# Start addresses of the tiles that TensorE reads, on multiples of 256 bytes, in a hybrid encoder block

## The chip, the core and the metric

The kernel runs on one core of one Trainium2 chip. The metric is the device time of one execution in microseconds, from runs of the whole kernel. The core has TensorE (PE, matmuls), VectorE (DVE), ScalarE (ACT), GpSimd (POOL) and SyncE (SP, which issues transfers). SBUF is the working memory: 128 partitions, each a run of bytes; a tile takes the same bytes in every partition. Matmuls write to PSUM. A matmul has a *stationary* operand, which a weight load (PEld in the profile) puts into the array, and a *moving* operand, which streams through it.

## The reference, cut to what matters

One layer on a sequence of 512 tokens with 1024 features, all in float32:

```
h      = rms_norm(x, g)
proj   = h @ w_in             # 1024 -> mLSTM q,k,v,o,gates | NA q,k,v | memory q | merge gates
y_ml   = mlstm_branch(...)                  # 4 heads of 128, two directions
y_na   = neighbourhood_attention(...)       # 8 heads of 64, an 8 x 64 grid
y_xa   = memory_cross_attention(...)        # 4 heads of 128, 256 memory tokens
merged = g_ml*(y_ml@w_br_ml) + g_na*(y_na@w_br_na) + g_xa*(y_xa@w_br_xa)
x      = x + merged @ w_out
x      = x + conv_glu_ffn(rms_norm(x), w_up, w_conv, b_conv, w_down)   # 1024 -> 2 x 2816 -> 1024
return rms_norm(x, final_norm_g)
```

Nearly all of the arithmetic is in the products with weights: `w_in`, the branch outputs, `w_out`, `w_up` and `w_down`.

## The kernel before

Activations are kept transposed: a tile holds 128 features by 512 tokens. For precision each float32 operand of a large product is split into a high part (`float32r`) and a low part, what is left; a product is then three matmuls, written by one helper, `mm3` (lines 207 to 209): high weights x high features, high weights x low features, low weights x high features. Each of the three loads its stationary operand anew.

Weights come in blocks of up to 1024 columns by a transfer into a `raw` tile (`wr`, three buffers), are split by ACT (line 189, high part) and DVE (line 190, low part) into tiles `wh` and `wl` (four buffers each, `HWD` = 544 floats a partition, that is 2176 bytes), one block ahead of TensorE. `proj` runs over the eight 128-feature slices of a contraction and calls `mm3` for each; the weights are stationary (128 x 128) and the features move (128 x 512). In the projection to mLSTM v and neighbourhood v (the blocks `tm`) and in the memory's v (`memv`) it is the other way: features or memory are stationary and weights move.

Features live in a ring of 15 `unit` buffers (`u`, `UNIT` = 2064 floats = 8256 bytes a partition), each with room for four tiles of 512. The input features, the merged features and those of the feed-forward stage take four units each. In all three, the first two units hold the high parts (eight tiles) and the last two the low parts, by lines such as

```
XH = [hx[k // 4][:, (k % 4) * S:(k % 4 + 1) * S] for k in range(KT)]
XL = [hx[2 + k // 4][:, (k % 4) * S:(k % 4 + 1) * S] for k in range(KT)]
```

Scratch tiles (`s`, seven buffers) are 516 floats. Constants (`ident` for transposes, `ones`, `onesr`) are single tiles in the pool `cp`. The row of norms, 512 reciprocal norms spread over all partitions (`rb_x` for the input, `rb_2` for the feed-forward stage, written at line 312), has two buffers. `rb_x` is read last in the gates of the third branch (line 1027).

The pools are laid out one behind the other in SBUF, in the order in which tiles are first made, on multiples of 32 bytes. So the sizes above decide at which byte each tile starts. The Tile framework orders each engine's work as the program is written.

Of the kernel before, what the change touches and what calls it, by code (L numbers as in the profile page):

```python
# [11 lines left out]
F32 = mybir.dt.float32  # L12
F32R = mybir.dt.float32r
# [4 lines left out]
P = 128  # L18
S = 512
D = 1024  # L20
KT = D // P
# [10 lines left out]
EPS = 1e-6  # L32
NEG = -1e30
BW = 1088
HWD = 544
UNIT = 2064
ROWS, GW = 8, 64
CW = (0, 8, 24, 32)
C_ML = (128.0 ** -0.5) / 4.0
# [67 lines left out]
def hybrid_block(ctx, tc, xg, xT, memT, wflat, vecs, gbias, nabias, outa, outb):  # L107
# [3 lines left out]
    cp = ctx.enter_context(tc.tile_pool(name="cp", bufs=1))  # L111
    wp = ctx.enter_context(tc.tile_pool(name="wp", bufs=3))
    up = ctx.enter_context(tc.tile_pool(name="up", bufs=NU))
    sp = ctx.enter_context(tc.tile_pool(name="sp", bufs=7))
# [7 lines left out]
    def nm(s):  # L122
        uid[0] += 1
        return f"{s}_{uid[0]}"

    def unit(dt=F32):
        return up.tile([P, UNIT], dt, tag="unit", name=nm("u"))

    def scr(n=512):
        return sp.tile([P, 516], F32, tag="scr", name=nm("s"))[:, :n]  # L130

    def tiny(n):
        return tp.tile([P, 32], F32, tag="tiny", name=nm("y"), bufs=12)[:, :n]
# [23 lines left out]
    def halves(i):  # L157
        n, c = BLOCKS[i][1], BCOLS[BLOCKS[i][0][0]](BLOCKS[i][0])
        k = n // c
        k0 = k if n <= HWD else (k + 1) // 2  # L160
        return c, [(0, k0)] + ([(k0, k)] if k0 < k else [])
# [10 lines left out]
    def emit_split(i):  # L172
        key, n = BLOCKS[i]
        r = raws.pop(i)
        c, hs = halves(i)
        split[i] = []
        for a, b in hs:
            m = (b - a) * c
            if key[0] == "dnl":
                h, l = lastw(4 * key[1] + a, m)  # L180
            else:
                h = wp.tile([P, HWD], F32R, tag="hi", name=nm("wh"), bufs=4)
                l = wp.tile([P, HWD], F32R, tag="lo", name=nm("wl"), bufs=4)
            for u, v in ((0, P), (P, 2 * P), (2 * P, m)) if i == 0 and a == 0 else ((0, m),):
                src = r[:, a * c + u:a * c + v]
                if i == 0 and a == u == 0:
                    V.tensor_copy(h[:, u:v], src)
                else:
                    A.activation(h[:, u:v], src, AF.Copy)  # L189
                V.tensor_tensor(l[:, u:v], src, h[:, u:v].bitcast(F32), op=ALU.subtract)  # L190
            for k in range(a, b):
                q = slice((k - a) * c, (k - a + 1) * c)
                split[i].append((h[:, q], l[:, q]))
# [62 lines left out]
    A.activation(cp.tile([P, 2], F32, name="first"), nc.const_aps.tensor(1.0, [P, 2], F32), AF.Tanh)  # L256
    SY.dma_start(vec, vecs)

    ident = cp.tile([P, P], F32, name="ident")
    make_identity(nc, ident)  # L260
    ones = cp.tile([P, P], F32, name="ones")
# [37 lines left out]
    def rstd_row(col, ntok, tag):  # L299

        nt = ntok // P
        ch, cl = tp.tile([P, 32], F32R, tag="tiny", name=nm("y"), bufs=12)[:, :nt], tiny(nt)
        A.activation(ch, col, AF.Copy)
        V.tensor_tensor(cl, col, ch.bitcast(F32), op=ALU.subtract)
        pb = atps()
        for n, c in enumerate((ch.bitcast(F32), cl)):
            dg = sp.tile([P, 516], F32R, tag="scr", name=nm("s"))[:, :ntok]
            for t in range(nt):
                V.tensor_scalar(dg[:, t * P:(t + 1) * P], ident, c[:, t:t + 1], None, op0=ALU.mult)
            PE.matmul(pb[:, :ntok], onesr, dg, start=n == 0, stop=n == 1)  # L310
        rb = cp.tile([P, ntok], F32, name=f"rb_{tag}", tag=f"rb{ntok}", bufs=2 if ntok == S else 1)
        A.activation(rb, pb[:, :ntok], AF.Copy)
        return rb


    hx = [unit(F32R) for _ in range(4)]
    XH = [hx[k // 4][:, (k % 4) * S:(k % 4 + 1) * S] for k in range(KT)]
    XL = [hx[2 + k // 4][:, (k % 4) * S:(k % 4 + 1) * S] for k in range(KT)]
    acc = cp.tile([P, S], F32, name="acc_x", tag="acc", bufs=1)

    ps_q = [mmps() for _ in range(4)]
# [1 line left out]
    def x_part(k):  # L323
        g = xgt[:, k:k + 1]
        if k > 0:
            split_act(XH[k], XL[k], xk[k], g)
        if k == 0:
            ha, hb = slice(0, S // 2), slice(S // 2, S)
            A.activation(XH[0][:, ha], xk[0][:, ha], AF.Copy, scale=g)
            A.activation(XH[0][:, hb], xk[0][:, hb], AF.Copy, scale=g)  # L330
        else:
# [37 lines left out]
    for k in range(KT):  # L369
# [75 lines left out]
    for c in range(3):  # L445
        n, nk = TMC[c], TMK[c]
        pss = [(mmps if c % 2 else atps)() for _ in range(NT)]
        for h in range(KT // nk):
            ws = weights(("tm", c, h))
            for t in range(NT):  # L450
                tsl = slice(t * P, (t + 1) * P)
                for k in range(nk):
                    kk = nk * h + k
                    ps = pss[t][:, :n]
                    mm3(ps, XH[kk][:, tsl], XL[kk][:, tsl], ws[k][0], ws[k][1], kk == 0, kk == KT - 1)
        for t in range(NT):
            ps = pss[t]
            if c == 0:
                V.scalar_tensor_tensor(Gt[:, t, :], ps[:, :16], rc[:, t:t + 1], gb, op0=ALU.mult, op1=ALU.add)
            if c < 2:  # L460
                o = 16 if c == 0 else 0
                A.activation(va[:, t, 2 * c:2 * c + 2, 0:128],
                             ps[:, o:o + 256].rearrange("p (h c) -> p h c", h=2), AF.Copy, scale=rcc[:, t:t + 1])
            if c > 0:

                nv = sp.tile([P, 516], F32R, tag="scr", name=nm("nv"))[:, :512]
                nvv = nv.rearrange("p (q y d) -> p q y d", q=2, y=4)
                pv = ps[:, n - 256:n].rearrange("p (q e d) -> p q e d", q=2, e=2)
                A.activation(nvv[:, :, 0:4:3, :], pv, AF.Copy, scale=rc[:, t:t + 1])
                for q in range(2):  # L470
                    V.scalar_tensor_tensor(nvv[:, q, 1:3, :], pv[:, q], rc[:, t:t + 1], nvv[:, q, 0:4:3, :].bitcast(F32),
                                           op0=ALU.mult, op1=ALU.subtract)
                G.dma_start(nav_d[t * P:(t + 1) * P, (c - 1) * 512:c * 512], nv)
# [389 lines left out]
    def xa_all(xq, mk, mv, yh, yl):  # L863
# [54 lines left out]
        q, k = prep(0)  # L918
        yield
        prev = None  # L920
        for h in range(4):
            sm = [scores(tq, q, k) for tq in range(2)]
            if prev:
                values(h - 1, *prev)
            yield
            v = prep_v(h)
            pT = [[sp.tile([P, 516], F32R, tag="scr", name=nm("s"))[:, :S] for _ in range(2)] for _ in range(2)]
            for tq in range(2):
                transposes(tq, sm[tq], pT)
            prev = (v, pT)  # L930
            if h < 3:
                q, k = prep(h + 1)
            yield
# [82 lines left out]
    for br in range(3):  # L1016
# [18 lines left out]
        for fp in range(4):  # L1035
# [6 lines left out]
            for i in range(2):  # L1042
                f = 2 * fp + i
# [8 lines left out]
                    V.tensor_tensor(mgv(f), mgv(f), tg[i], op=ALU.add)  # L1052
            step(RATE[br])
    mhu = [unit(F32R) for _ in range(4)]
    GH = [mhu[k // 4][:, (k % 4) * S:(k % 4 + 1) * S] for k in range(KT)]
    GL = [mhu[2 + k // 4][:, (k % 4) * S:(k % 4 + 1) * S] for k in range(KT)]
    for k in range(KT):
        split_act(GH[k], GL[k], mgv(k), 0.5)

# [1 line left out]
    x2u = [unit(), unit()]  # L1061
    x2 = [x2u[f // 4][:, (f % 4) * S:(f % 4 + 1) * S] for f in range(KT)]
    h2 = [unit(F32R) for _ in range(4)]
    HH = [h2[k // 4][:, (k % 4) * S:(k % 4 + 1) * S] for k in range(KT)]
    HL = [h2[2 + k // 4][:, (k % 4) * S:(k % 4 + 1) * S] for k in range(KT)]
    acc2 = cp.tile([P, S], F32, name="acc_2", tag="acc", bufs=1)
    for f in range(KT):
        xr = scr()
        SY.dma_start(xr, xT[f])
        ps = proj(("out", f), GH, GL)  # L1070
        V.tensor_tensor(x2[f], ps, xr, op=ALU.add)
        split_act(HH[f], HL[f], x2[f], vcol("ffn_g", f))
        if f == 0:
# [128 lines left out]
    for hh in range(2):  # L1202
# [159 lines left out]
```

## Time and profile before

| | |
|---|---|
| median of 3 runs | 896.2 us (895.94 to 896.33) |
| the profiled execution's own time | 895.66 us |
| its span, first to last instruction | 893.9 us |
| matmul instructions | 4350 |
| bytes moved by transfers | 99.68 MB |
| granted TensorE clock | 1.00 |

How to read it: busy time on TensorE is modelled, since matmuls are pipelined; two of them overlap in the profile, so that the mean of one is longer than the distance from one start to the next. `PEld` is the weight load, which runs beside the matmul before it. In the groups, a name such as `mm<-u,wh` says that a PSUM tile is written from a feature unit and a high weight tile; `x1022` is the count, then the busy time in us and the mean of one in ns.

### The profile page before, as it was taken

The page shows a single profiled execution, that of the slowest core. Times are in us where ns is not written, and L with a number is a line of the kernel's source. Part 1 is how long each engine was busy: PE and PEld are TensorE (multiplying, and loading weights), DVE is VectorE, ACT ScalarE, POOL GpSimd, SP SyncE. Part 2 cuts the span into 40 slices and gives each one's busy share as a digit, 9 for nine tenths or more (in the row PEclk, how much of TensorE's full clock was granted, in tenths as well). Part 3 has the DMA queues.
Part 4 walks back from the last instruction along what each step waited for, and adds up shares of the span by engine and source line. Part 5 has one row for each costly group of instructions (what it writes and reads, how often), then busy time and mean ns, then how long its engine had stood idle before and what let it go on. Part 6 is the DMA issues. An engine that isn't in the chain of part 4 may idle for free.

```text
span 893.9 us, 12254 instructions
## 1 busy us (share of the span) xinstructions
PE 887.6 (99%) x4350; PEld 741.5 (83%) x4350; DVE 578.1 (65%) x1181; ACT 451.7 (51%) x951; POOL 135.3 (15%) x209
## 2 busy tenths in 40 slices
PE   9999999999999999999999999999999999999997
PEld 7898889888888888888888888888888888888887
DVE  6794686766567657998676548766633566667433
ACT  7353556644556548888644435444422344444442
POOL 0101100000070660510000211111100011111010
PEclk9999999999999999999999999999999999999999
DMA  7224643422242443533223322222223222222412
GB/s 269 97 84 126 203 131 118 166 103 87 71 124 91 117 119 118 150 122 119 105 95 107 142 106 94 95 95 95 73 98 105 102 95 96 98 96 82 138 34 95
DMA packets 39293, 99.68 MB, mean 112 GB/s; under 512 B 5688, under 2 KB 14008, under 8 KB 39232
## 3 DMA queue, kind: packets, MB, share of 16 engines
q1 hardware_dynamic: 31440, 92.32, 30.0%
q0 software_dynamic: 7360, 6.32, 3.2%
q8 instruction: 34, 0.56, 0.3%
q10 hardware_dynamic: 432, 0.26, 0.1%
q14 instruction: 27, 0.22, 0.1%
HBM read 94.67 MB, written 4.21 MB: 111 GB/s over the span
## 4 chain that ended last, share of the span: by engine, by line
PE 98%; ACT 1%; issue 0%; DVE 0%; POOLq 0%; POOL 0%; DVEq 0%
PE mm L208 29%; PE mm L207 29%; PE mm L209 29%; PE at L207 2%; PE at L208 2%; PE at L209 2%; PE at L816 1%; PE at L670 1%; PE at L797 1%; PE at L635 1%; PE at L672 1%; PE at L651 0%; PE at L904 0%; PE at L779 0%; PE at L778 0%
## 5 line engine op out<-in xcount | busy, mean ns | idle before, releaser
L207 PE MATMUL mm<-u,wh 128*128 128x512 f32 (+1 forms) x1076 | 420.0, 390 | 0.0
L208 PE MATMUL mm<-u,wh 128*128 128x512 f32 (+1 forms) x1076 | 418.0, 388 | 0.0
L209 PE MATMUL mm<-u,wl 128*128 128x512 f32 (+1 forms) x1076 | 416.6, 387 | 0.0
L189 ACT ACTIVATE wh<-wr 128x512 fp32r<-128x512 f32 (+3 forms) x299 | 185.5, 622 | 266.8 <-PE mm L208 218.5
L190 DVE TENSOR_TENSOR wl<-wr,wh 128x512 fp32r<-128x512 f32 (+3 forms) x300 | 206.7, 690 | 110.7 <-ACT wh L189 106.0
L209 PEld LDWEIGHTS mm<-u,wl 128*128 128x128 f32 x1076 | 202.2, 188 | 43.5
L207 PEld LDWEIGHTS mm<-u,wh 128*128 128x128 f32 x1076 | 202.3, 188 | 42.7
L208 PEld LDWEIGHTS mm<-u,wh 128*128 128x128 f32 x1076 | 202.4, 188 | 42.0 <-DVE u L214 0.3
L1231 POOL TENSOR_TENSOR s<-s,rb 128x512 f32<-128x512 f32 x22 | 37.4, 1699 | 257.7 <-DVE s L1230 249.6
L483 POOL DMA_DIRECT2D u<-nav_d x128 | 62.5, 556 | 74.8 <-PE at L816 34.7
L213 ACT ACTIVATE u<-s 128x512 fp32r<-128x512 f32 x26 | 16.4, 631 | 53.8 <-DVE s L1234 53.6
L1234 DVE TENSOR_TENSOR s<-mm,s 128x512 f32<-128x512 f32 x22 | 15.2, 690 | 22.5 <-POOL s L1231 22.5
L403 ACT ACTIVATE s<-pad,vec 128x512 f32<-128x512 f32 x30 | 24.4, 814 | 8.5 <-DVE pad L401 8.5
L1078 POOL TENSOR_TENSOR acc<-acc,s 128x512 f32<-128x512 f32 x7 | 9.1, 1300 | 128.1 <-ACT s L1077 128.1
L214 DVE SCALAR_TENSOR_TENSOR u<-s,u 128x512 fp32r<-128x512 f32 x26 | 18.0, 692 | 14.3 <-ACT u L213 14.0
L404 DVE SCALAR_TENSOR_TENSOR s<-pad,vec,s 128x512 f32<-128x512 f32 x30 | 22.5, 751 | 6.1 <-ACT s L403 6.1
L1230 DVE SCALAR_TENSOR_TENSOR s<-s,s 128x512 f32<-128x512 f32 x22 | 15.2, 692 | 13.4 <-ACT s L1229 13.3
L405 DVE SCALAR_TENSOR_TENSOR s<-pad,vec,s 128x512 f32<-128x512 f32 x30 | 22.5, 751 | 0.9
L1229 ACT ACTIVATE s<-s 128x512 f32<-128x512 f32 x22 | 13.9, 632 | 15.5 <-DVE s L1228 15.4
L401 DVE TENSOR_TENSOR pad<-mm,rb 128x512 f32<-128x512 f32 x22 | 15.1, 692 | 9.5 <-PE mm L209 9.5
L207 PE MATMUL mm<-wh,u 128*128 128x512 f32 x48 | 19.1, 398 | 0.0
L209 PE MATMUL mm<-wh,u 128*128 128x512 f32 x48 | 18.9, 394 | 0.0
(295 smaller groups left out, 1019.2 us busy)
## 6 DMA issues: line engine op xcount, KB each, us to landing
wr<-wflat SPq DMA_DIRECT2D x141, 512.0 KB, 3.2
nab<-nabias SPq DMA_DIRECT2D x16, 256.0 KB, 2.6
u<-nav_d POOLq DMA_DIRECT2D x128, 32.0 KB, 2.7
s<-xT SPq DMA_DIRECT2D x15, 256.0 KB, 3.8
wr<-wflat SPq DMA_DIRECT2D x14, 192.0 KB, 2.3
nav_d<-nv POOLq DMA_DIRECT2D x8, 256.0 KB, 2.4
R<-rd SPq DMA_DIRECT2D x8, 256.0 KB, 3.8
wr<-wflat SPq DMA_DIRECT2D x2, 544.0 KB, 3.2
```

The costliest lines, as they stand in the source:

```text
L189: A.activation(h[:, u:v], src, AF.Copy)
L190: V.tensor_tensor(l[:, u:v], src, h[:, u:v].bitcast(F32), op=ALU.subtract)
L207: PE.matmul(ps, lh, rh, start=start, stop=False)
L208: PE.matmul(ps, lh, rl, start=False, stop=False)
L209: st["mm"] = PE.matmul(ps, ll, rh, start=False, stop=stop).ins
L213: A.activation(h, src, AF.Copy, scale=scale)
L214: V.scalar_tensor_tensor(l, src, scale, h.bitcast(F32), op0=ALU.mult, op1=ALU.subtract)
L403: A.activation(t1, pad[:, 0:512], AF.Identity, scale=vcol(w, i), bias=vcol(b, i))
L404: V.scalar_tensor_tensor(t1, pad[:, 1:513], vcol(w, n + i), t1, op0=ALU.mult, op1=ALU.add)
L405: V.scalar_tensor_tensor(t1, pad[:, 2:514], vcol(w, 2 * n + i), t1, op0=ALU.mult, op1=ALU.add)
L483: G.dma_start(vw[r * 32:(r + 1) * 32, i * 256:(i + 1) * 256], nav_v[hf, r, CW[b]:CW[b] + 32, hp * 256:(hp + 1) * 256])
L1231: G.tensor_tensor(c, c, rb2, op=ALU.mult)
```

## The change: where tiles start

Four things are changed:

- Sizes are raised so that every buffer of the rings is a multiple of 256 bytes: `UNIT` from 2064 to 2112 floats (8448 bytes), the tiles `wh` and `wl` from 544 to 576 floats (2304 bytes; only 544 are used), scratch from 516 to 512 floats (2048 bytes).
- An unused tile `gap` of 16 floats ahead of `ident` moves what follows by 64 bytes.
- In the three groups of four units, high and low parts alternate: units 0 and 2 hold the high parts, 1 and 3 the low parts.
- The row of norms has one buffer of 2048 bytes where it had two, which makes room for the larger tiles.

```
+GAP = 16
-HWD = 544
-UNIT = 2064
+HWD, HWT = 544, 576
+UNIT = 2112
...
     def scr(n=512):
-        return sp.tile([P, 516], F32, tag="scr", name=nm("s"))[:, :n]
+        return sp.tile([P, S], F32, tag="scr", name=nm("s"))[:, :n]
...
-                h = wp.tile([P, HWD], F32R, tag="hi", name=nm("wh"), bufs=4)
-                l = wp.tile([P, HWD], F32R, tag="lo", name=nm("wl"), bufs=4)
+                h = wp.tile([P, HWT], F32R, tag="hi", name=nm("wh"), bufs=4)
+                l = wp.tile([P, HWT], F32R, tag="lo", name=nm("wl"), bufs=4)
...
+    cp.tile([P, GAP], F32, name="gap")
     ident = cp.tile([P, P], F32, name="ident")
...
-        rb = cp.tile([P, ntok], F32, name=f"rb_{tag}", tag=f"rb{ntok}", bufs=2 if ntok == S else 1)
+        rb = cp.tile([P, ntok], F32, name=f"rb_{tag}", tag=f"rb{ntok}", bufs=1)
...
-    XH = [hx[k // 4][:, (k % 4) * S:(k % 4 + 1) * S] for k in range(KT)]
-    XL = [hx[2 + k // 4][:, (k % 4) * S:(k % 4 + 1) * S] for k in range(KT)]
+    XH = [hx[k // 4 * 2][:, (k % 4) * S:(k % 4 + 1) * S] for k in range(KT)]
+    XL = [hx[k // 4 * 2 + 1][:, (k % 4) * S:(k % 4 + 1) * S] for k in range(KT)]
...
```

The same two lines change for the merged features (`GH`, `GL`) and for those of the feed-forward stage (`HH`, `HL`). Three more lines that make scratch tiles take the size 512.

Where the tiles then start in a partition, in bytes of the two built programs, with what is left over a multiple of 256:

| tile | before | over 256 | after | over 256 |
|---|---|---|---|---|
| `ident` | 12224 | 192 | 12288 | 0 |
| `wh` buffers | 44224, 46400, 48576, 50752 | 192, 64, 192, 64 | 42240, 44544, 46848, 49152 | 0 |
| `wl` buffers | 52928, 55104, 57280, 59456 | 192, 64, 192, 64 | 51456, 53760, 56064, 58368 | 0 |
| input, high | 61632 and 168960 | 192 and 0 | 60672 and 170496 | 0 |
| input, low | 177216 and 160704 | 64 and 192 | 178944 and 162048 | 0 |
| memory, high and low | 119424 and 111168 | 128 and 64 | 119808 and 111360 | 0 |
| feed-forward, high | 177216 and 168960 | 64 and 0 | 178944 and 170496 | 0 |
| feed-forward, low | 61632 and 127680 | 192 and 192 | 60672 and 128256 | 0 |
| scratch `s` | 185472, 187552, ... (steps of 2080) | 128, 160, ... | 187392, 189440, ... (steps of 2048) | 0 |
| tiles `R`, `H`, `E`, `X` | 205664, ... (steps of 2048) | 96 | 207360, ... (steps of 2048) | 0 |

A slice of 128 floats (one weight tile) is 512 bytes and one of 512 floats (one feature tile) is 2048 bytes, so slices of such a tile keep what is left over 256. The list of instructions of each engine, their order and the semaphores that they wait for are the same in both programs.

More of the change, by code (lines that the diff above doesn't have):

```diff
@@ L306, in rstd_row @@
         for n, c in enumerate((ch.bitcast(F32), cl)):
-            dg = sp.tile([P, 516], F32R, tag="scr", name=nm("s"))[:, :ntok]
+            dg = sp.tile([P, S], F32R, tag="scr", name=nm("s"))[:, :ntok]
             for t in range(nt):
@@ L464, in hybrid_block @@
             if c > 0:
-                nv = sp.tile([P, 516], F32R, tag="scr", name=nm("nv"))[:, :512]
+                nv = sp.tile([P, S], F32R, tag="scr", name=nm("nv"))[:, :512]
                 nvv = nv.rearrange("p (q y d) -> p q y d", q=2, y=4)
@@ L926, in xa_all @@
             v = prep_v(h)
-            pT = [[sp.tile([P, 516], F32R, tag="scr", name=nm("s"))[:, :S] for _ in range(2)] for _ in range(2)]
+            pT = [[sp.tile([P, S], F32R, tag="scr", name=nm("s"))[:, :S] for _ in range(2)] for _ in range(2)]
             for tq in range(2):
@@ L1054, in hybrid_block @@
     mhu = [unit(F32R) for _ in range(4)]
-    GH = [mhu[k // 4][:, (k % 4) * S:(k % 4 + 1) * S] for k in range(KT)]
-    GL = [mhu[2 + k // 4][:, (k % 4) * S:(k % 4 + 1) * S] for k in range(KT)]
+    GH = [mhu[k // 4 * 2][:, (k % 4) * S:(k % 4 + 1) * S] for k in range(KT)]
+    GL = [mhu[k // 4 * 2 + 1][:, (k % 4) * S:(k % 4 + 1) * S] for k in range(KT)]
     for k in range(KT):
@@ L1063, in hybrid_block @@
     h2 = [unit(F32R) for _ in range(4)]
-    HH = [h2[k // 4][:, (k % 4) * S:(k % 4 + 1) * S] for k in range(KT)]
-    HL = [h2[2 + k // 4][:, (k % 4) * S:(k % 4 + 1) * S] for k in range(KT)]
+    HH = [h2[k // 4 * 2][:, (k % 4) * S:(k % 4 + 1) * S] for k in range(KT)]
+    HL = [h2[k // 4 * 2 + 1][:, (k % 4) * S:(k % 4 + 1) * S] for k in range(KT)]
     acc2 = cp.tile([P, S], F32, name="acc_2", tag="acc", bufs=1)
```

## The prediction

> **What bounds the kernel now.** I read the first part of the page (busy shares), then the chain of work that ended last, then the waits of TensorE, then the groups by shape, and at last the order in time of single matmuls.
>
> ```profile
> span 893.9 us, 12254 instructions
> PE 887.6 (99%) x4350; PEld 741.5 (83%) x4350; DVE 578.1 (65%) x1181; ACT 451.7 (51%) x951; POOL 135.3 (15%) x209
> PE 98%; ACT 1%; issue 0%; DVE 0%; POOLq 0%; POOL 0%; DVEq 0%
> PE mm L208 29%; PE mm L207 29%; PE mm L209 29%; PE at L207 2%; PE at L208 2%; PE at L209 2%; PE at L816 1%; PE at L670 1%; PE at L797 1%; PE at L635 1%; PE at L672 1%; PE at L651 0%; PE at L904 0%; PE at L779 0%; PE at L778 0%
> ...
> PE at L237 <- PEq L1353: 0.8, 1, 0.8
> PE at L816 <- DVE w L805: 0.2, 1, 0.2
> ```
>
> TensorE is busy for 99% of the span, it makes up 98% of the chain, and the list of what it waited for has two entries that add to 1.0 us. Everything else waits for it. 87% of the chain are the three matmuls of one helper, lines 207 to 209 (high weights with high features, high with low, low with high). The groups by shape say how many there are:
>
> ```profile
> L207 PE MATMUL mm<-u,wh 128*128 128x512 f32 x1022 | 404.5, 396 | 0.0
> L208 PE MATMUL mm<-u,wh 128*128 128x512 f32 x1022 | 402.7, 394 | 0.0
> L209 PE MATMUL mm<-u,wl 128*128 128x512 f32 x1022 | 401.5, 393 | 0.0
> L207 PE MATMUL mm<-wh,u 128*128 128x512 f32 x48 | 19.1, 398 | 0.0
> L207 PE MATMUL at<-u,wh 128*128 128x512 f32 x16 | 6.4, 398 | 0.0
> ```
>
> With the rows of L208 and L209 that go with the last two (48 and 16 again) that is 3 x (1022 + 48 + 16) = 3258 matmuls of 512 columns. A mean of about 394 ns is not what one costs: the next one starts before this one's modelled end. What one costs is the distance from start to start, and that is read from the order in time. In the feed-forward stage:
>
> ```profile
> 540.00:700.00 160.00, 160.00 (x694) 1.00 0.28 93
> ```
>
> 694 matmuls in 160 us are 230.5 ns each, at a granted clock of 1.00. So **the time of this kernel is 3258 times some 231 ns (753 us) plus the shorter matmuls**, and one nanosecond of spacing is worth 3.26 us, or 0.36%.
>
> **What the change can touch.** The two programs hold the same instructions, in the same order and with the same waits, on all five engines. What differs is the byte in each partition at which a tile starts. No instruction is added or removed, no transfer is moved, so the only term is what a start address does to the duration of an instruction, above all to the spacing of matmuls. That the address does something is seen where the same loop runs over tiles at other addresses. The projection to v and k (tiles "tm" 1) has the feature tiles as stationary operand and the weights as moving one. Its weights start at 192 or 64 bytes above a multiple of 256 throughout. Its features are at 192 (high) and 64 (low) in the first half, and at 0 (high) and 192 (low) in the second; in the value projection of the memory, with weights at the same places, they are at 128 and 64. The rows below are L207's, six matmuls apart; each figure is a start:
>
> ```profile
> 66.97 0.39 PE L207 MATMUL mm<-wh,u 128*128 128x512 f32 x1
> 68.36 0.39 PE L207 MATMUL mm<-wh,u 128*128 128x512 f32 x1
> 69.76 0.39 PE L207 MATMUL mm<-wh,u 128*128 128x512 f32 x1
> ...
> 78.05 0.39 PE L207 MATMUL mm<-wh,u 128*128 128x512 f32 x1
> 79.42 0.39 PE L207 MATMUL mm<-wh,u 128*128 128x512 f32 x1
> 80.80 0.39 PE L207 MATMUL mm<-wh,u 128*128 128x512 f32 x1
> ...
> 164.78 0.40 PE L207 MATMUL mm<-wh,u 128*128 128x512 f32 x1
> 166.19 0.40 PE L207 MATMUL mm<-wh,u 128*128 128x512 f32 x1
> 167.60 0.40 PE L207 MATMUL mm<-wh,u 128*128 128x512 f32 x1
> ```
>
> Twelve matmuls took 2.79 us with features at 192 and 64 (232.5 ns each), 2.75 us at 0 and 192 (229.2 ns), and 2.82 us at 128 and 64 (235.0 ns). The stage whose high features lie on a multiple of 256, and with them two of each three weight loads, is the fastest of the three, by 3.3 and by 5.8 ns a matmul. That is the evidence for a gain. The feed-forward stage gives evidence that points elsewhere. There the features move and the weights are loaded; high features lie at 64 and low ones at 192 in the first half of a projection, at 0 and 192 in the second; weights lie at 64 in one projection and at 192 in the next:
>
> ```profile
> 591.65 0.40 PE L207 MATMUL mm<-u,wh 128*128 128x512 f32 x1
> 593.05 0.40 PE L207 MATMUL mm<-u,wh 128*128 128x512 f32 x1
> ...
> 594.44 0.39 PE L207 MATMUL mm<-u,wh 128*128 128x512 f32 x1
> 595.81 0.39 PE L207 MATMUL mm<-u,wh 128*128 128x512 f32 x1
> ...
> 597.21 0.39 PE L207 MATMUL mm<-u,wh 128*128 128x512 f32 x1
> 598.59 0.39 PE L207 MATMUL mm<-u,wh 128*128 128x512 f32 x1
> ...
> 599.96 0.39 PE L207 MATMUL mm<-u,wh 128*128 128x512 f32 x1
> 601.35 0.39 PE L207 MATMUL mm<-u,wh 128*128 128x512 f32 x1
> ```
>
> Six matmuls each. With weights at 64: 1.40 us for high features at 64, 1.37 us at 0. With weights at 192: 1.38 us at 64, 1.39 us at 0. So 233.3, 228.3, 230.0 and 231.7 ns. The slowest is the one where the high features and the weights that load beside them lie at the same distance from a multiple of 256. A multiple of 256 for the moving operand helps in one projection and hurts in the next.
>
> A rule of the Trainium skill speaks against any effect. "SBUF — State Buffer", section "Who interferes with whom", gives TensorE two read ports of its own, one for the moving operand and one for weight loads, and says that it waits for no other engine; the section "Operand start alignment" of the same page calls alignment a matter of what is legal, and timed nothing. By that rule the sum of this change is 0 us. The rows above do not agree: 228.3 to 235.0 ns for one shape. A second page of the Trainium skill, "TensorE: Matmul & The Clock Gate", section "Wait — 56ns, not 53.3ns?", gives 215.7 ns from start to start at 512 columns; no stretch of this trace shows it (228.3 ns is the least above), and reaching it everywhere would be, as an estimate from that page, some 50 us.
>
> **The sum.** (a) *512-column matmuls.* After the change features, weights and scratch tiles all stand on multiples of 256. The nearest row is the middle stage of the first table, against the same loop at 192 and 64, which at 232.5 ns is close to the kernel's average: -3.3 ns. 3258 x -3.3 ns = **-10.8 us**. Bounds: the 128-and-64 stage against the 0-and-192 one, 3258 x -5.8 = -18.9 us; and the other side, all at the spacing of the equal-distance row (233.3 instead of 230.5), 3258 x 2.8 = +9.1 us. I take the middle stage because its two of three aligned loads are the nearest thing to a kernel with all of them aligned.
>
> (b) *Shorter matmuls.* They make up most of the rest of TensorE's time. Before the change one group has all three operands at the same distance from a multiple of 256 (96 bytes), as all will have after:
>
> ```profile
> L207 PE MATMUL at<-X,X x16: 280/282/287, 254.5 to 304.1; 128*128 128x256 f32 x16
> L208 PE MATMUL at<-X,X x16: 279/282/287, 254.6 to 304.2; 128*128 128x256 f32 x16
> ...
> L207 PE MATMUL at<-wh,u 128*128 128x256 f32 x32 | 9.0, 281 | 0.0
> L797 PE MATMUL at<-ident,s 128*128 128x128 f32 x64 | 10.3, 274 | 0.0
> ```
>
> 282 ns against 281 ns at mixed distances: 1 ns, on some 600 matmuls 0.6 us. For the transposes (274 ns) the scratch tiles stand at several distances already. I take 0, with +-0.6 us.
>
> (c) *Hi and lo alternating.* It picks other buffers of the ring for the same tiles. In the built program the high and low tile of a pair then lie 0 or 256 bytes apart, counted in multiples of 512, where they lay 128 to 448 apart. The rows above have no such pair; it is inside the bounds of (a).
>
> (d) *One buffer for the row of norms.* The second row now takes the first one's place and must wait for its last reader.
>
> ```profile
> L1027 DVE TENSOR_TENSOR u<-mm,rb_x x8: 673/692/692, 404.0 to 451.5; 128x512 f32<-128x512 f32 x8
> L312 ACT ACTIVATE rb<-at x1: 599/599/599, 535.8 to 535.8; 128x512 f32<-128x512 f32 x1
> ```
>
> The last reader started at 451.5 us, the second row is written at 535.8 us: 84 us of cover, cost 0. Were that cover gone, the 0.6 us of the write would stand on ACT, behind it the weights' split.
>
> (e) *ACT, DVE, POOL and the transfers.* They too read and write at new places. ACT is busy for 51% and DVE for 65%, and TensorE waited 0.2 us for them in all, so that a change of a few per cent in either is hidden. If TensorE gets 1% faster they keep up: their splits wait for TensorE, not the other way. Cost 0.
>
> Sum: -10.8 us against the profiled execution's own 895.66 us (a span of 893.9 us and 1.8 us around it), which gives 884.9 us. The median of the runs is 896.2 us, 0.5 us above that execution, so the forecast for a median is **885.3 us**.
>
> **The rivals.** *Collision of equal distances.* Moving operand and weight load now start at the same place within 256 bytes, for every matmul. For it: the slowest feed-forward row (233.3 ns) is the one with that property, and the group with all three operands alike is 1 ns slower than its like. Against it: in the first half of the v-and-k stage the high weights at 192 load features at 192 and are only average (232.5 ns). Price: 3258 x 2.8 ns = 9.1 us at most, 3258 x 1 ns = 3.3 us by the group; so 899 to 905 us. It decides as soon as the mean spacing rises above the 230.5 ns of now. *No effect.* Gains and losses with the neighbour's address cancel, as they do now from stage to stage: 895 to 898 us. The rule cited above from the Trainium skill's "SBUF — State Buffer", "Who interferes with whom", implies this result. For it: the mean over long stretches is 230.5 ns though addresses differ widely. Against it: after the change there is one distance, not a mixture, and single distances differ by up to 6.7 ns. *A larger gain.* Each weight load and each moving read that starts on a multiple of 256 saves on its own: all three loads aligned instead of two of three, 3.3 x 3/2 = 5.0 ns, to 5.8 ns: -16 to -19 us, 877 to 880 us. *The change does not do what it says.* In the built program the features of the neighbourhood attention still start at 32, 96 and 128 above a multiple (windows of columns), the weights of the 272-column block step by 64, and the tile of log gates and the sum for the memory norm are off as well; these are few matmuls, so that this case takes under 1 us from the others.
>
> **How the numbers follow.** Forecast (881 to 889 us) 0.40; larger gain (below 881) 0.12; no effect 0.18; collision 0.30. Faster by over 0.2% is 0.40 + 0.12 = 0.52, within 0.2% (about what a measurement of this kernel can tell from no change) 0.18, slower 0.30. Since cases of both signs hold much, the range reaches from 875 us (the 18.9 us bound and a little more) to 904 us (most of the collision case); the forecast alone would be 881 to 889 us.
>
> **What would show it.** In the changed kernel's order in time, the starts of L207 in the feed-forward stage should be about 0.683 us apart (3 x 227.7 ns) where they were 0.692 on average, the stretch from 540 to 700 us should hold some 700 matmuls instead of 694, and the v-and-k stage should have one spacing in both halves. 0.70 us between those starts is the collision. TensorE should still wait about 1 us in all, and the two rows of norms should show no wait on ACT. The prediction is wrong if spacings depend on more than the distance within 256 bytes, such as the place within 512 or the address of the tile that moved before, since nothing in the trace of before has all operands on multiples of 256.

## The result: 884.3 us, and the profile after

The changed kernel takes 884.32 us (median; runs from 884.02 to 884.48), the kernel before 896.12 us on the same chip (895.94 to 896.33). The ratio is 0.9868, 95% interval 0.9851 to 0.9885: faster by 11.8 us. The forecast was 885.3 us. Every median here and below is of runs at a granted clock of 0.998 to 1.00; a few runs at 0.655 to 0.851 took 969 to 1256 us and are left out.

The first part of the page of the changed kernel (busy time and share of the span by engine, with the number of instructions), and from the fourth part the shares of the chain that ended last, by engine and line:

```profile
span 882.7 us, 12254 instructions
...
PE 876.2 (99%) x4350; PEld 741.3 (84%) x4350; DVE 574.7 (65%) x1181; ACT 451.8 (51%) x951; POOL 135.8 (15%) x209
...
PE mm L209 28%; PE mm L211 28%; PE mm L210 28%; PE at L209 2%; PE at L210 2%; PE at L211 2%; PE at L673 1%; PE at L819 1%; PE at L800 1%; PE at L638 1%; PE at L675 1%; PE at L654 0%; PE at L907 0%; ACT s L791 0%; PE at L239 0%
```

The picture is the same as before, 11.2 us shorter. The same 12254 instructions run, TensorE is busy for 99% and makes the chain. (The three matmuls of the helper now stand two lines further down, at L209 to L211.) What TensorE waited for, in the list of its waits in the changed kernel (total, times, longest):

```profile
PE at L239 <- PEq L1356: 0.8, 1, 0.8
PE at L819 <- DVE w L808: 0.4, 2, 0.3
```

That is 1.2 us, against 1.0 us before: no wait was removed, and none to speak of added. So the time must have gone out of the matmuls themselves. The groups by shape (busy time, mean of one; both by the modelled ends, so that they show the direction and not the price):

```profile
L209 PE MATMUL mm<-u,wh 128*128 128x512 f32 x1022 | 401.3, 393 | 0.0
L211 PE MATMUL mm<-u,wl 128*128 128x512 f32 x1022 | 398.5, 390 | 0.0
L210 PE MATMUL mm<-u,wh 128*128 128x512 f32 x1022 | 398.5, 390 | 0.0
L209 PE MATMUL mm<-u,wh 128*128 128x256 f32 x54 | 15.6, 289 | 0.0
L211 PE MATMUL mm<-u,wl 128*128 128x256 f32 x54 | 15.3, 283 | 0.0
L210 PE MATMUL mm<-u,wh 128*128 128x256 f32 x54 | 15.3, 283 | 0.0
...
L209 PE MATMUL at<-wh,u 128*128 128x256 f32 x32 | 9.1, 283 | 0.0
```

The three groups of 1022 matmuls had 404.5, 402.7 and 401.5 us and now have 1198.3 us together, 10.4 us less in modelled durations. What one costs is the distance from its start to the next one's. Taken over all matmuls of both traces, the 3258 matmuls of 512 columns went from 232.5 to 228.9 ns on average, 3.6 ns each and 11.7 us in all; those of 256 columns together cost 0.8 us more, the rest 0.2 us less. That sums to 11.1 of the 11.2 us. The order in time shows it matmul by matmul. In the feed-forward stage of the changed kernel (start, duration):

```profile
591.36 0.39 PE L209 MATMUL mm<-u,wh 128*128 128x512 f32 x1
...
592.04 0.39 PE L209 MATMUL mm<-u,wh 128*128 128x512 f32 x1
...
595.44 0.39 PE L209 MATMUL mm<-u,wh 128*128 128x512 f32 x1
```

Eighteen matmuls take 595.44 - 591.36 = 4.08 us, 226.7 ns each, where single places of the kernel before had 228.3 to 235.0 ns. From one L209 to the next it is 0.68 us. The two halves of the v-and-k stage and the value projection of the memory, which had 232.5, 229.2 and 235.0 ns, now all have it:

```profile
67.07 0.39 PE L209 MATMUL mm<-wh,u 128*128 128x512 f32 x1
...
69.79 0.39 PE L209 MATMUL mm<-wh,u 128*128 128x512 f32 x1
...
77.95 0.39 PE L209 MATMUL mm<-wh,u 128*128 128x512 f32 x1
...
80.67 0.39 PE L209 MATMUL mm<-wh,u 128*128 128x512 f32 x1
```

Each pair is twelve matmuls apart: 2.72 us in both halves, and the memory's stage has the same (164.27 to 166.99 us). The stretch from 540 to 700 us (the first pair of figures is PE, with its number of matmuls in parentheses):

```profile
540.00:700.00 160.00, 160.00 (x708) 132.48 (x707) 91.54 (x140) 62.45 (x102) 16.56 (x10) 1.00 0.29 99
```

708 matmuls instead of 694, at the same granted clock of 1.00. A faster clock is not the reason.

The number is the forecast one. Whether the reason is the forecast one, this profile cannot say: all addresses are multiples of 256 now, *and* all are alike. The forecast rested on the first, and its main rival priced the second as a loss. The experiments separate the two.

### The profile page after: what moved, and what is told of

It reads as the page before. It is cut to its first block, busy times and chain, and to the rows that moved or that the text cites. A ratio compares the mean times of both kernels' runs of the same rounds, so it can differ in the third digit from the quotient of the medians.

```text
span 882.7 us, 12254 instructions
## 1 busy us (share of the span) xinstructions
PE 876.2 (99%) x4350; PEld 741.3 (84%) x4350; DVE 574.7 (65%) x1181; ACT 451.8 (51%) x951; POOL 135.8 (15%) x209
## 4 chain that ended last, share of the span: by engine, by line
PE 96%; ACT 2%; DVE 1%; issue 1%; POOLq 0%; POOL 0%; DVEq 0%
PE mm L209 28%; PE mm L211 28%; PE mm L210 28%; PE at L209 2%; PE at L210 2%; PE at L211 2%; PE at L673 1%; PE at L819 1%; PE at L800 1%; PE at L638 1%; PE at L675 1%; PE at L654 0%; PE at L907 0%; ACT s L791 0%; PE at L239 0%
## 5 line engine op out<-in xcount | busy, mean ns | idle before, releaser
L209 PE MATMUL mm<-u,wh 128*128 128x512 f32 (+1 forms) x1076 | 416.9, 388 | 0.0
L211 PE MATMUL mm<-u,wl 128*128 128x512 f32 (+1 forms) x1076 | 413.8, 385 | 0.0
L192 DVE TENSOR_TENSOR wl<-wr,wh 128x512 fp32r<-128x512 f32 (+3 forms) x300 | 203.5, 680 | 105.1 <-ACT wh L191 98.7
L211 PEld LDWEIGHTS mm<-u,wl 128*128 128x128 f32 x1076 | 202.2, 188 | 40.5 <-DVE wl L192 0.7
L209 PEld LDWEIGHTS mm<-u,wh 128*128 128x128 f32 x1076 | 202.4, 188 | 38.5 <-ACT wh L191 0.4
L791 ACT ACTIVATE s<-s,y 128x256 f32<-128x256 f32 x32 | 16.0, 501 | 6.1 <-DVE y L788 5.9
L209 PE MATMUL mm<-wh,u 128*128 128x512 f32 x48 | 19.0, 396 | 0.0
```

What stands on the lines that cost most here:

```text
L209: PE.matmul(ps, lh, rh, start=start, stop=False)
L211: st["mm"] = PE.matmul(ps, ll, rh, start=False, stop=stop).ins
```

## The experiments

Each kernel is the changed kernel with the edit shown, unless said otherwise; each time stands against the kernel before, on the same chip. "Sum over three" is the distance from one first matmul of the helper to the next: 680 ns in the changed kernel. Where no rows are shown, sums and means are worked out from the starts of all matmuls in that kernel's trace. In the edited kernels the helper's lines shift by up to five.

### Everything 64 bytes further, and the alternation undone

```
-GAP = 16
+GAP = 32
```

> The changed kernel with every tile behind the unused one moved up by another 64 bytes: all operands at 64 over a multiple of 256, distances between them as in the change. Theory A, multiples of 256 count in themselves: the gain is lost, 893 to 900 us, L209 starts about 0.693 us apart on average. Theory D, only the distance between moving and stationary operand counts, and it is zero: 884.3 us within 0.8, starts 0.680 apart. Theory U, any distance will do if it is the same everywhere: 884.3 us too.

The alternation undone, in the same way for `GH`, `GL` and `HH`, `HL`:

```
-    XH = [hx[k // 4 * 2][:, (k % 4) * S:(k % 4 + 1) * S] for k in range(KT)]
-    XL = [hx[k // 4 * 2 + 1][:, (k % 4) * S:(k % 4 + 1) * S] for k in range(KT)]
+    XH = [hx[k // 4][:, (k % 4) * S:(k % 4 + 1) * S] for k in range(KT)]
+    XL = [hx[2 + k // 4][:, (k % 4) * S:(k % 4 + 1) * S] for k in range(KT)]
...
```

> The changed kernel with high and low parts again in the first two and the last two units; sizes and starts as in the change. If the alternating adds nothing (theories A, D and U alike): 884.3 us within 0.8. If the place of the low part within 512 bytes of the high one counts: 886 us or more.

With everything at 64 above a multiple of 256: 884.41 us, ratio 0.9873 (0.9858 to 0.9888). Without the alternation: 884.91 us, ratio 0.9877 (0.9863 to 0.9892). The stretch from 540 to 700 us of the shifted kernel:

```profile
540.00:700.00 160.00, 160.00 (x707) 132.49 (x706) 91.54 (x139) 62.44 (x101) 16.56 (x10) 1.00 0.30 99
```

Not one tile of the first kernel that TensorE reads in this stage lies on a multiple of 256, and it is as fast. So the multiple has no part in the gain; that step of the prediction falls. The order of high and low parts in the ring has none that these runs can tell either (the two intervals and the changed kernel's own lie over each other).

### The weights moved away from the features

Features stay on multiples of 256; an unused tile ahead of the weight tiles moves them by 32, 64, 128 or 192 bytes, and one behind them keeps the rest in place. For 64 bytes:

```
+    wp.tile([P, 16], F32, name="wgap", tag="wgap", bufs=1)
...
+                if i == 0 and a == 0:
+                    wp.tile([P, 48], F32, name="wend", tag="wend", bufs=1)
```

> The changed kernel with the high and low weight tiles alone moved to 64 over a multiple of 256; features, scratch and all else stay on multiples. Theory A: the 512-column matmuls lose the half of the gain that belongs to the weight's side, 888 to 892 us. Theory D, distance zero counts: no better than the kernel before, 893 to 900 us. Theory U, one distance everywhere: 884.3 us within 0.8.

> The same with the weight tiles at 128 over a multiple of 256. Theory A: 888 to 892 us, as at 64. Theory D: 890 to 900 us, and not the same as at 64, since the distance is another. Theory U: 884.3 us within 0.8.

> The weight tiles alone at 192 over a multiple of 256, so that the moving tile stands 64 above the weights (modulo 256) where it stood 64 below them with weights at 64. If the sign counts, as the v-and-k stage with weights at 64 says (there weights move and stand 64 above the features, and three matmuls took 0.687 us instead of 0.700): 884.3 + 3258 x 2.3 ns = 892 us, 889 to 894. If only the size of the distance counts: 903 us, as at 64.

> The weight tiles alone at 32 over a multiple of 256. If a distance below 64 bytes is as good as none: 884.3 us within 0.8. If each byte of distance counts: 888 us or more, up to the 903 us seen at 64.

| weights above features | time, us | ratio to before (95%) | matmuls in 540 to 700 us |
|---|---|---|---|
| 0 (the change) | 884.32 | 0.9868 (0.9851 to 0.9885) | 708 |
| 32 | 903.16 | 1.0083 (1.0065 to 1.0101) | 687 |
| 64 | 902.91 | 1.0079 (1.0064 to 1.0094) | 687 |
| 128 | 901.04 | 1.0059 (1.0042 to 1.0076) | 691 |
| 192 | 891.23 | 0.9948 (0.9933 to 0.9964) | 701 |

The distance between the two operands alone is worth 18.8 us, more than the whole change. One distance for all is not enough (theory U falls), and with the weights at 32, 64 or 128 nothing is left of the gain (theory A had half of it left). At 64 and 128 the kernels are even slower than theory D had named, 900 us at most: a wrong distance throughout costs more than the mixture of before. The distance has a direction: counted within 256 bytes, 192 above is the same as 64 below, and costs 6.9 us where 64 above costs 18.6. In the v-and-k stage the two operands change places (weights move, features are loaded), so there the same kernels must show the opposite. In the order in time of the kernel with weights at 64:

```profile
67.95 0.39 PE L211 MATMUL mm<-wh,u 128*128 128x512 f32 x1
...
73.44 0.39 PE L211 MATMUL mm<-wh,u 128*128 128x512 f32 x1
...
600.02 0.40 PE L211 MATMUL mm<-u,wh 128*128 128x512 f32 x1
...
604.92 0.39 PE L211 MATMUL mm<-u,wh 128*128 128x512 f32 x1
```

and of the kernel with weights at 192:

```profile
68.00 0.39 PE L211 MATMUL mm<-wh,u 128*128 128x512 f32 x1
...
73.59 0.39 PE L211 MATMUL mm<-wh,u 128*128 128x512 f32 x1
...
600.10 0.39 PE L211 MATMUL mm<-u,wh 128*128 128x512 f32 x1
...
604.90 0.39 PE L211 MATMUL mm<-u,wh 128*128 128x512 f32 x1
```

The first pair of rows of each kernel is 24 matmuls apart, the second 21. Weights at 64: 5.49 / 24 = 228.8 ns where they move, 4.90 / 21 = 233.3 ns where they are loaded. Weights at 192: 5.59 / 24 = 232.9 ns and 4.80 / 21 = 228.6 ns. So a moving operand 64 bytes above the loaded one costs some 2 ns a matmul over equal starts, 64 below it costs 6.2 to 6.6, whichever tile plays which part.

### Only the low parts moved

A matmul runs while the next one's weights load, so "alike" could mean alike to its own weights or to those that load beside it. In the helper (high weights with high features, high with low, low with high) moving low weights *and* low features by 64 keeps the distance to the weights that load beside at zero everywhere, and changes the distance to the own weights in two of three matmuls (the other low features as `hx` here). Moving the low features alone leaves two of three matmuls at distance zero to their own weights.

```
+LO = 16
...
+            lw.extend(unit(F32R) if i < 2 else unit(F32R)[:, LO:] for i in range(4))
...
+                if i == 0 and a == 0:
+                    wp.tile([P, LO], F32, name="wgap", tag="wgap", bufs=1)
...
+    hx[1], hx[3] = hx[1][:, LO:], hx[3][:, LO:]
...
```

> Low weights and low features alone moved to 64 over a multiple of 256, high ones stay on multiples. Each moving tile then keeps distance zero from the weights that load while it streams (those of the next matmul), but two of three matmuls have distance 64 from the weights they use, and from the moving tile before. Theory B, the distance to the weights that load beside it counts: 884.3 us within 0.8. Theory O, the distance to the weights in use counts, or theory M, the distance from one moving tile to the next counts: 890 to 900 us.

In the second kernel only the slices of the low features (`[:, LO:]`) are kept:

> Low features alone moved to 64 over a multiple of 256, all weights and high features on multiples. Of each three matmuls the middle one (low features moving) is at distance 64 both from the weights in use and from those that load beside it. Theories B and O: a part of the gain is lost, by 2.3 to 6.7 ns on 1035 matmuls of 512 columns, 886.7 to 891.5 us. Theory A (multiples of 256 in themselves), which has fallen, would say the same; theory M: 890 us or more.

Low weights and features at 64: 896.42 us, ratio 1.0007 (0.9997 to 1.0016). Low features alone: 898.83 us, ratio 1.0035 (1.0022 to 1.0048). The stretch from 540 to 700 us, of the first and then of the second:

```profile
540.00:700.00 160.00, 160.00 (x694) 130.12 (x693) 98.55 (x140) 63.22 (x102) 15.48 (x11) 1.00 0.30 93
```

```profile
540.00:700.00 160.00, 160.00 (x692) 129.45 (x691) 100.26 (x141) 63.88 (x103) 14.96 (x11) 1.00 0.30 94
```

The first kernel has distance zero to the weights that load beside, and all of the gain is gone: that distance alone is not what counts. The second missed its expectation by 7 us and more. Its bounds came from one matmul of three being at another distance; in fact the whole gain went, and 3 us more. In that stretch all three matmuls of the helper are slow, by the starts 231.2, 232.2 and 232.6 ns on average against 226.0, 227.0 and 227.0 in the changed kernel, although two of them have operands that start alike. What one matmul costs is therefore not a matter of its own two operands only. Theory M (the step from one moving tile to the next) had named both results, 890 us or more; it cannot be all either, since with all weights at 64 every moving tile starts alike and the kernel is slow.

### TensorE alone

A kernel in which nothing but TensorE works, on constant data. Each group of 48 matmuls writes to one tile that bears the group's name; the features `X` and weights `W` are read at chosen distances:

```
    def triples(name, hx, lx, hw, lw, n=512):
        ops = []
        for i in range(N // 3):
            k = i % 4
            ops += [(ws(0, k, hw), xs(0, k, hx, n), n), (ws(0, k, hw), xs(1, k, lx, n), n),
                    (ws(1, k, lw), xs(0, k, hx, n), n)]
        run(name, ops)

    def rolling(name, s, m):
        run(name, [(ws(i // 4 % 2, i % 4, s(i) % 256), xs(i // 4 % 2, i % 4, m(i) % 256, 512), 512) for i in range(N)])
```

> The whole computation is left out, outputs are zeros: 39 groups of 48 matmuls on constant data, each group into one PSUM tile named after it, no other engine at work. w0b to w252b: features at 0, weights 0 to 252 bytes above a multiple of 256. all16b to all64b: both moved alike. half0b to half192b: weights at 0 to 192, 256 columns. follow_q, lowx_q, loww_q: low weights and low features, low features, low weights at 64. own64z: both step by 64, distance zero to a matmul's own weights, 64 to those loading beside it; beside64z: the other way round; movroll64z, wroll64z: moving operand or weights step alone; the same with 128. bf0b to bf128b: bfloat16. Theory 1, TensorE's own two reads hinder each other by their starts: w0b 226 to 227 ns from start to start, w32b and w64b 232 to 234, w192b 228 to 230, all16b to all64b as w0b. Theory 2, other engines are needed: all groups within 1 ns. Forms of theory 1: own distance counts: own64z and own128z as w0b, beside64z 232 or more; distance beside counts: the other way round (the low pair moved together, which lost the gain, speaks against it); a change of start on the moving side costs: movroll64z slow, wroll64z not, or the reverse for loads; all reads must start alike: own, beside, movroll, wroll all 2 ns or more above w0b. half groups: 117 to 120 ns, half0b slowest. bfloat16: no row here speaks of it; under 1 ns between the four.

The order in time, one row for a group: start of the first, and the time from there to the end of the last.

```profile
19.05 11.05 PE L47 MATMUL w0b<-X,W 128*128 128x512 f32 x48
29.94 11.32 PE L47 MATMUL w4b<-X,W 128*128 128x512 f32 x48
...
85.75 11.35 PE L47 MATMUL w64b<-X,W 128*128 128x512 f32 x48
96.94 11.40 PE L47 MATMUL w96b<-X,W 128*128 128x512 f32 x48
...
130.54 11.16 PE L47 MATMUL w192b<-X,W 128*128 128x512 f32 x48
...
163.87 11.13 PE L47 MATMUL w240b<-X,W 128*128 128x512 f32 x48
174.84 11.36 PE L47 MATMUL w248b<-X,W 128*128 128x512 f32 x48
186.04 11.05 PE L47 MATMUL w252b<-X,W 128*128 128x512 f32 x48
196.92 11.25 PE L47 MATMUL all16b<-X,W 128*128 128x512 f32 x48
208.01 11.07 PE L47 MATMUL all32b<-X,W 128*128 128x512 f32 x48
218.92 11.07 PE L47 MATMUL all64b<-X,W 128*128 128x512 f32 x48
229.82 5.91 PE L47 MATMUL half0b<-X,W 128*128 128x256 f32 x48
235.57 5.82 PE L47 MATMUL half64b<-X,W 128*128 128x256 f32 x48
...
252.58 11.27 PE L47 MATMUL follow_q<-X,W 128*128 128x512 f32 x48
263.69 11.30 PE L47 MATMUL lowx_q<-X,W 128*128 128x512 f32 x48
...
285.91 11.23 PE L47 MATMUL own64z<-X,W 128*128 128x512 f32 x48
296.98 11.27 PE L47 MATMUL beside64z<-X,W 128*128 128x512 f32 x48
308.09 11.29 PE L47 MATMUL movroll64z<-X,W 128*128 128x512 f32 x48
319.22 11.29 PE L47 MATMUL wroll64z<-X,W 128*128 128x512 f32 x48
330.35 11.13 PE L47 MATMUL own128z<-X,W 128*128 128x512 f32 x48
...
374.55 10.53 PE L47 MATMUL bf0b<-XB,WB 128*128 128x512 bf16 x47
...
395.28 10.52 PE L47 MATMUL bf64b<-XB,WB 128*128 128x512 bf16 x47
```

From a row's time the last matmul's own 0.39 us (0.28 at 256 columns, 0.38 in bfloat16) is taken off, and the rest divided by 47. The whole kernel's figures stand beside, from the sums over three between 540 and 700 us, that of `w192b` from the rows above (by the sums it is 228.9):

| group | ns a matmul, alone | in the whole kernel |
|---|---|---|
| `w0b` (all alike) | 226.8 | 226.7 (the change) |
| `w64b` | 233.2 | 233.3 |
| `w192b` | 229.1 | 228.6 |
| `all64b` | 227.2 | 226.7 (everything at 64) |
| `follow_q` | 231.5 | 231.1 |
| `lowx_q` | 232.1 | 232.0 |

TensorE alone shows what the whole kernel shows, to within half a nanosecond. No other engine and no transfer is needed for it: theory 2 falls. Of the forms of theory 1, distance zero to the own weights while the start steps by 64 gives 230.6 ns (`own64z`), zero to the weights beside 231.5 (`beside64z`), one operand stepping alone 231.9 (either). Each single relation loses most of the gain; only the form in which *all* reads must start alike is left of those put up. Its bound of 2 ns was missed once: `own128z`, stepping by 128, is 1.7 ns above `w0b`. Also, "alike" is too simple in two ways. Weights 4 bytes below the features are as good as equal ones (`w252b`, 226.8 ns), 4 above are not (`w4b`, 232.6), nor are 8 below (`w248b`, 233.4), while 16 below (`w240b`, 228.5) is better than that again. So the pace does not follow the distance smoothly. And all at 16 is slower (231.1 ns) than all at 0, 32 or 64; in the table of starts of the two kernels every tile lies on a multiple of 32, so this has no part in the result.

The length and the type matter. At 256 columns equal starts are the slower ones: (5.91 - 0.28) / 47 = 119.8 ns (`half0b`) against 117.9 (`half64b`). In bfloat16 the start changes next to nothing: 216.0 and 215.7 ns (one record of each of these groups is missing; the rows span 48 matmuls).

### One half of the change alone

Feature tiles aligned, weight tiles left at 2176 bytes:

```
-HWD, HWT = 544, 576
+HWD, HWT = 544, 544
```

> The change with the weight tiles left 2176 bytes long, as before: feature and scratch tiles start on multiples of 256, weights by turns on a multiple and 128 bytes above one. Theory 1 (a matmul is fast only where its own reads and those of its neighbours all start alike; the group of weights at 128 showed 232.4 ns, the one at 0 226.7 ns): blocks with weights at 0 keep sums of 680 ns over three matmuls, blocks at 128 show about 697; the mean over all is some 2.5 to 3 ns above the changed kernel, 892 us (890 to 896), so that the features alone bring about a third of the gain. Rival (each aligned tile saves on its own, and the features are one of the two sides of each matmul): half of the gain everywhere, sums of 686 to 688 throughout, 890 us.

Weight tiles aligned, feature tiles left at 8256 bytes:

```
-UNIT = 2112
+UNIT = 2064
```

> The change with the feature tiles left 8256 bytes long, as before: weight and scratch tiles start on multiples of 256, a feature tile 64 bytes further than the one before it in the ring, counted within 256. Theory 1: high and low features differ mostly from each other and from the weights, so that next to no block has all reads alike; by the single groups (226.7 ns at 0, 228.8 at 64 above the weights, 232.4 at 128, 233.3 at 192) and the group with low features elsewhere (232.1 ns) the mean is 230 to 232 ns against 231.0 before, 893 to 900 us: the weights alone bring nothing. Rival (each aligned tile saves on its own): half of the gain, 890 us.

Features alone: 895.36 us, ratio 0.9993 (0.9983 to 1.0002). Weights alone: 899.15 us, ratio 1.0033 (1.0022 to 1.0045). Neither half brings anything; the second is a small loss. This is the plainest evidence that the gain belongs to the relation between tiles, and not to any tile. The rival of the expectations (each aligned tile saves its share, 890 us) is out by 5 us and more. Theory 1's range held both times (890 to 896 and 893 to 900), but with the features it named 892, 3.4 us too low. The order in time of the kernel with aligned features shows both paces side by side. In the feed-forward stage the weight tiles of one projection (eight slices, 24 matmuls) lie at 0 and those of the next at 128, in turn:

```profile
599.84 0.39 PE L209 MATMUL mm<-u,wh 128*128 128x512 f32 x1
...
602.57 0.40 PE L209 MATMUL mm<-u,wh 128*128 128x512 f32 x1
...
605.36 0.39 PE L209 MATMUL mm<-u,wh 128*128 128x512 f32 x1
```

These rows are twelve matmuls apart each: 2.73 us (227.5 ns a matmul) up to the end of one projection, then 2.79 us (232.5 ns) from the start of the next. Over the whole trace the sums (those under 720 ns) average 692.1 ns (230.7 a matmul). With weights on multiples of 256 they average 683 to 689 by place instead of 680, with weights at 128 they average 697 to 700, against 697 where all weights lie there. The expectation had counted the single groups and nothing for the change from one to the other. The starts show that change: of the eight sums of a projection at 0, six are 680 ns as in the changed kernel, the first, behind weights at 128, is some 692 and the last, ahead of them, some 686.

## Why the prediction was right in its number and wrong in its reason

**What bounds the kernel.** Right. The spacing of the 512-column matmuls sets the time: 3.6 ns on each of 3258 are 11.7 us, more than the 11.2 us by which the span became shorter.

**(a) 512-column matmuls, -3.3 ns for -10.8 us.** The size was nearly right (-3.6 ns, -11.7 us), the reason wrong. The prediction took the stage with high features "on a multiple of 256, and with them two of each three weight loads" as the fast one because of the multiple. The kernel with everything at 64 (ratio 0.9873) shows that the multiple is worth nothing, and the kernels with half of the tiles aligned (0.9993 and 1.0033) that aligned tiles don't save one by one. That a mixed stage stood 3.3 ns below the one it was compared with, about what equal starts now bring, is luck: in that stage moving weights at 192 or 64 met loads at 0 and 192. The rival of a larger gain rested on the same multiple and falls with it.

**The collision rival, 0.30.** Its relation was the right one to look at and its sign was wrong. "Moving operand and weight load now start at the same place within 256 bytes" is what brings the gain. The prediction read the slowest feed-forward row (233.3 ns, weights and high features both at 64) as an equal-distance row. But the low features of that stretch lay at 192, and the kernel with only the low features elsewhere (898.83 us) shows that one odd operand of four is enough to lose everything. The evidence for the rival was a row in which not all reads were alike, and the one group that had all alike (the `X` tiles, 282 against 281 ns) had 256 columns, where equal starts do cost 1.9 ns.

**(b) Shorter matmuls, 0 with +-0.6 us.** Outside its bound by a little: by the starts, those of 256 columns cost 0.8 us, which nearly cancels the 0.9 us by which (a) was too small. The modelled durations show where. At 256 columns the group `mm<-u,wh` went from 287, 282 and 280 to 289, 283 and 283 ns, six for three; 54 of these are 0.3 us, the 44 of `mm<-u,u` (also six for three) 0.3 us and the 32 of `at<-wh,u` (281 to 283, six again) 0.2 us. The transposes kept their time, as taken.

**(c) Alternation: inside the bounds.** Right: 884.91 us without it, 884.32 with it, with ratios (0.9877 and 0.9868) whose intervals lie over each other.

**(d) One buffer for the row of norms, 0.** Right. The rows of its last reader and of its write in the changed kernel:

```profile
L1030 DVE TENSOR_TENSOR u<-mm,rb_x x8: 675/691/692, 400.4 to 447.4; 128x512 f32<-128x512 f32 x8
...
L315 ACT ACTIVATE rb<-at x1: 602/602/602, 530.4 to 530.4; 128x512 f32<-128x512 f32 x1
```

83 us lie between them, and no wait of ACT on that reader appears among its waits.

**(e) Other engines, 0.** Right: TensorE waits 1.2 us in all. VectorE's 279 weight splits of 512 columns went from 700 to 689 ns on average. This is not a matter of where tiles start: without those over 800 ns the mean is 688 ns in both kernels, and the difference is three splits of 1.8 us in the kernel before, each while GpSimd multiplied two tiles. Nothing came of it, since VectorE is not the bound:

```profile
L192 DVE TENSOR_TENSOR wl<-wr,wh 128x512 fp32r<-128x512 f32 x279 | 191.8, 689 | 88.2 <-ACT wh L191 81.9 <-PE at L313 2.0 <-PE at L782 0.9
```

**The rules cited.** By the Trainium skill, "SBUF — State Buffer", section "Who interferes with whom", TensorE's moving operand and its weight loads come through two independent ports; by that, as the prediction put it, the change is worth nothing. The runs do not agree: TensorE alone goes from 226.8 to 233.2 ns when the weights move by 64 bytes. The other page of the Trainium skill, "TensorE: Matmul & The Clock Gate", section "Wait — 56ns, not 53.3ns?", gives 215.7 ns; the bfloat16 groups agree (215.7 and 216.0), while no group or stage of 512 columns here that is in this kernel's type has a mean below 226.7.

**The warning at the end.** "Spacings depend on more than the distance within 256 bytes, such as ... the address of the tile that moved before": this is how it is, as far as the runs tell. The prediction had named it as the sign that would make it wrong: its number held, its reason did not.

**The last sum.** 884.9 and 0.5 us are 885.4 us, not 885.3; nothing hangs on it.

What stays open is how the reads hinder each other. The runs show which arrangements are fast. They do not show what in TensorE's path to memory makes 4 bytes below as good as equal and 8 bytes below as bad as 64 above.

## What to carry to other kernels

Where a kernel is one long row of 512-column matmuls in this type (fp32r in the rows of the splits), give *all* their operands, high and low parts, moving and loaded, the same start within 256 bytes (0, 32 and 64 served here, 16 did not); aligning one kind of tile alone brings nothing. Measure the pace as the distance between starts, not as a duration: 680 ns against 693 to 700 for three shows at once whether it holds. And when evidence for a rule comes from stages that differ in several addresses, look for one in which all agree before putting a sign on it; where there is none, as here, time that case by itself, as the groups of 48 matmuls do.

## What the runs showed of the hardware

- The start addresses of TensorE's two operands alone move the pace of 512-column matmuls in this kernel's type from 226.8 to 234.3 ns (`w0b` and `w96b`), with no other engine at work, and in the full kernel's feed-forward stage from 226.7 to 233.3 ns (884.3 to 903.2 us).
- The order counts: moving operand 64 bytes above the loaded one 228.6 to 229.1 ns, 64 below 232.9 to 233.3.
- At 256 columns it is the other way round (119.8 ns with equal starts, 117.9 at 64), and in bfloat16 there is none to speak of (216.0 and 215.7).
- One operand of four at another start slows its neighbours too: with the low features alone moved, all three matmuls of the helper take 231 to 233 ns.
- VectorE's subtraction of two 512-column operands (279 of them) took 687 to 689 ns on average wherever the tiles started, but for those over 800 ns. Three of these in the kernel before, and 18 of 279 with weights at 64, took 1.8 us, each while GpSimd multiplied two tiles; the changed kernel has none, and others beside that multiplication kept their pace. What decides it is open.
